# Value projections of two attention mixers in halves of 256 columns, two accumulator banks each, and earlier key fills

## The chip, the cores and the metric

The kernel runs as one program on one core of a Trainium2 chip. The metric is the device time of one execution in microseconds (us). The profile names the engines PE (TensorE: matrix products), PEld (its loads of the stationary operand), DVE (VectorE), ACT (ScalarE), POOL (GpSimd) and SP (SyncE, which issues most DMAs).

## The reference

A trunk of two layers works on x (512 positions, 1024 channels) with a memory of 256 positions, all in float32. Cut to what matters here:

```python
# layer 0, the first mixer
proj = rms_norm(x) @ attn_w_in            # 1024 -> 3080 columns
fq, fk, fv, ff, dq, dk, dv = split(proj)  # fv: 512 columns, 8 heads of 64
p = softmax(causal(fq @ fk.T / 8 + F[:, None] - F[None, :]))   # F = cumsum(log_sigmoid(ff))
fox_out = p @ fv
d_out = rms_norm((softmax(mask(dq1 @ dk1.T)) - lam * softmax(mask(dq2 @ dk2.T))) @ dv)
x = x + concat(fox_out, d_out) @ attn_w_out
# layer 1, the second mixer
qk, v, ig, fg, og = split(rms_norm(x) @ mlstm_w_in)   # v: 1024 columns, 4 heads of 256
q, k = split(silu(causal_depthwise_conv(qk)))         # 4 heads of 128
num, den = gated_causal_sums(q, k, v, ig, fg)         # chunkwise in the reference
h = rms_norm(num / max(abs(den), exp(-m)))            # by heads
x = x + (h * sigmoid(og)) @ mlstm_w_out
# both layers, behind the mixer
x = x + memory_cross_attention(rms_norm(x), rms_norm(mem))
x = x + conv_ffn(rms_norm(x))                         # 1024 -> 2 x 2816 -> 1024
```

A last rms_norm follows. The output is 512 x 1024.

## The kernel before

**Precision.** Each operand of a matrix product is split into a high and a low part (`hi = cast(v)`, `lo = v - hi`), and a product is three matmuls: high by high, high by low, low by high. In projections with channels in the partitions these are lines 388, 389 and 390 (`mm3`), in the value projections (tokens in the partitions, `p_proj_tok`) lines 450, 451 and 452. Each weight tile is 128 x 1024 (512 KB). SP loads it into `raw` (three buffers), ACT casts it to `wh`, DVE subtracts to `wl`. Nearly every operation of ACT and DVE is recorded at line 310, the wrapper that keeps an engine's operations in order, so the names of its tiles tell them apart.

**Order.** The two mixers are written as items for a planner (class `Plan`, line 86). An item has a priority (lower goes first), items that it depends on, and resources that it takes and frees: two banks for scores ("s"), two for weighted sums and transposes ("w"), four accumulator banks ("acc"), three weight slots ("wt"), and buffers such as "v" and "qk". The plan keeps a clock of ACT and DVE and lists the items one by one; in that order the instructions go out on each engine, and each engine keeps to it.

**First mixer** (`mix0`, line 876). The differential attention's four heads and the forgetting attention's eight heads, the latter in four pairs `p_` with priorities 50, 60, 70, 80. A pair's q and k projections (`p_qk`) give `qa` and `ka`; scores (lines 798 and 799; `kb` carries a bias part) go to an "s" bank; the softmax is POOL's bias, DVE's sums (`sm`) and ACT's exponentials, DVE scales `x` by 1/sum; PE transposes x into `w` (line 831) and a copy makes `pt`; line 1068 multiplies pt by the values v. The values of all eight heads are one projection 512 wide, `p_values` (line 847) with priority 49: eight steps over the channels of 12 matmuls 128 x 512, in four accumulator banks, one for each 128 tokens. A pair's weighted sum waits for all four.

Then come the output projection (`wo0`, eight blocks of 24 matmuls of 512 columns, which read `mh`/`ml`, `ka`, `qa`, the parts of the mixer's output) with priority 100, and the key fills (`p_fill`, line 1140): two blocks of the memory's keys, for the cross-attention that follows, four weights with 24 matmuls of 256 columns each, with priority 99 and not before 210 us on the planner's clock.

**Second mixer** (from line 2100). Gates, four heads with priorities 10, 20, 30, 40. A head's q and k blocks (24 matmuls of 512 each) go through a convolution on DVE and ACT (`hs`, `cv`, `th`) to `q`, `ql`, `k`, `kl`; scores `s<-q,k`, masked to `at`; denominators by `w<-hsq,ones` (line 2254); numerators `w<-at,v` (line 2275) go to `num`; their squares `hsq` are summed on PE (line 547), and the root comes back through a DMA as `hrb`, by which DVE scales num. The gates' columns are transposed at line 2132 (`s<-ident,cv`). The values are two projections of 512 columns (two heads each) in four banks: the first with priority 2, ahead of all heads, the second with 31, and a head's numerators wait for its projection, `ves[h // 2]`.

The rest of each layer (cross-attention, ConvFFN) is ordered by another class and isn't touched.

## Time and profile before

| | |
|---|---|
| median of 3 runs | 1406.63 us (1406.47 to 1407.09) |
| profiled execution, its own time | 1407.05 us |
| its span | 1404.9 us |
| granted TensorE clock | 1.00 |
| busy: PE, PEld | 1390.2 us (99%), 1265.2 us (90%) |
| busy: DVE, ACT, POOL | 1186.4 us (84%), 874.4 us (62%), 146.8 us (10%) |
| DMA | 211.06 MB, mean 150 GB/s |

The profile is of one execution, and its own time is 0.42 us above the median; the span is the part from the first to the last recorded instruction. [...] In square brackets behind a row stands how long the engine idled before it and what released it. "out<-in" gives the tiles by their names in the program, "128*128 128x512" the shape of the stationary operand and of the result.

### The profile page before, as it was taken

How to read it: one execution, taken by the hardware profiler on the slowest of the kernel's cores; microseconds unless marked ns; L12 is line 12 of the kernel's file. 1: busy time of each engine (PE TensorE's matmuls, PEld its weight loads, DVE VectorE, ACT ScalarE, POOL GpSimd, SP SyncE). 2: the span in 40 equal slices, each digit the busy share in tenths (PEclk: the TensorE clock that was granted, in tenths of full speed). 3: DMA queues.
4: the chain of work that ended last, by engine and by line, in shares of the span. 5: the costliest groups of instructions: out<-in, count | busy, mean ns of one | idle time of the engine just before them, and what ended most of it. 6: DMA issues, size and time to landing. Idle time of an engine off the chain costs nothing.

```text
span 1404.9 us, 23512 instructions
## 1 busy us (share of the span) xinstructions
PE 1390.2 (99%) x8876; PEld 1265.2 (90%) x8876; DVE 1186.4 (84%) x2042; ACT 874.4 (62%) x1486; POOL 146.8 (10%) x213
## 2 busy tenths in 40 slices
PE   9999999999999999999999999999999999999998
PEld 8888878899899999999888888989989999999997
DVE  7787786888799999999768876678878999999984
ACT  6797565666576665666456664456656866565555
POOL 0002230010011111011001120001000111110000
PEclk9999999999999999999999999999999999999999
DMA  6225324765567787674333332367464878776522
GB/s 207 91 53 154 117 68 151 246 188 158 158 145 191 211 199 187 151 200 106 86 108 105 129 98 83 120 188 240 136 185 114 196 201 204 182 185 168 154 66 81
DMA packets 80544, 211.06 MB, mean 150 GB/s; under 512 B 8640, under 2 KB 8640, under 8 KB 80432
## 3 DMA queue, kind: packets, MB, share of 16 engines
q1 hardware_dynamic: 63520, 165.02, 36.3%
q0 software_dynamic: 15904, 43.44, 17.7%
q8 instruction: 69, 1.13, 0.3%
q10 hardware_dynamic: 1008, 1.12, 0.2%
q14 instruction: 43, 0.35, 0.1%
HBM read 203.20 MB, written 6.34 MB: 149 GB/s over the span
## 4 chain that ended last, share of the span: by engine, by line
PE 85%; DVE 8%; ACT 3%; issue 2%; DMA 1%; POOL 1%; SPq 0%; POOLq 0%; DVEq 0%; ACTq 0%
PE acc L388 16%; PE acc L390 16%; PE acc L389 16%; PE w L388 4%; PE w L389 4%; PE w L390 4%; PE s L388 3%; PE s L390 3%; PE s L389 3%; PE acc L451 2%; PE acc L452 2%; PE acc L450 2%; DVE wl L310 1%; DVE qc L310 1%; PE w L2275 1%
## 5 line engine op out<-in xcount | busy, mean ns | idle before, releaser
L310 ACT CAST wh<-raw 128x1024 fp32r<-128x1024 f32 (+2 forms) x217 | 222.0, 1026 | 160.9 <-PE acc L389 76.4
L310 DVE TENSOR_TENSOR wl<-raw,wh 128x1024 fp32r<-128x1024 f32 (+2 forms) x217 | 259.6, 1198 | 39.2 <-ACT wh L310 37.9
L388 PE MATMUL acc<-xh,wh 128*128 128x256 f32 (+1 forms) x704 | 228.7, 325 | 0.0
L390 PE MATMUL acc<-xh,wl 128*128 128x256 f32 (+1 forms) x704 | 227.4, 323 | 0.5 <-DVE wl L310 0.5
L389 PE MATMUL acc<-xl,wh 128*128 128x256 f32 (+1 forms) x704 | 227.1, 323 | 0.0
L390 PEld LDWEIGHTS acc<-xh,wl 128*128 128x128 f32 x704 | 134.4, 191 | 9.3 <-DVE wl L310 0.9
L388 PEld LDWEIGHTS acc<-xh,wh 128*128 128x128 f32 x704 | 134.5, 191 | 7.6
L389 PEld LDWEIGHTS acc<-xl,wh 128*128 128x128 f32 x704 | 134.5, 191 | 7.5
L310 DVE SCALAR_TENSOR_TENSOR qc<-va,vec,qc 128x512 f32<-128x512 f32 x176 | 131.8, 749 | 6.9 <-ACT qc L310 4.0
L389 PE MATMUL acc<-f,k 128*128 128x256 f32 x336 | 92.5, 275 | 0.0
L390 PE MATMUL acc<-f,k 128*128 128x256 f32 x336 | 92.5, 275 | 0.0
L388 PE MATMUL acc<-f,k 128*128 128x256 f32 x336 | 92.5, 275 | 0.0
L310 ACT ACTIVATE qc<-va,vec 128x512 f32<-128x512 f32 x88 | 71.1, 812 | 19.2 <-DVE q L310 9.5
L388 PE MATMUL w<-q,wh 128*128 128x512 f32 x208 | 79.1, 380 | 0.6 <-ACT qc L310 0.6
L390 PE MATMUL w<-q,wl 128*128 128x512 f32 x208 | 78.9, 379 | 0.0
L389 PE MATMUL w<-q,wh 128*128 128x512 f32 x208 | 78.9, 379 | 0.0
L310 ACT ACTIVATE u<-acc 128x256 f32<-128x256 f32 x96 | 36.4, 379 | 68.1 <-PE acc L390 66.4
L390 PE MATMUL acc<-mem,wl 128*128 128x256 f32 (+1 forms) x236 | 73.8, 313 | 1.1 <-DVE wl L310 1.1
L388 PE MATMUL acc<-mem,wh 128*128 128x256 f32 (+1 forms) x236 | 73.9, 313 | 0.1
L389 PE MATMUL acc<-mem,wh 128*128 128x256 f32 (+1 forms) x236 | 73.7, 312 | 0.0
L310 DVE TENSOR_TENSOR x<-acc,x 128x512 f32<-128x512 f32 (+1 forms) x43 | 28.0, 653 | 47.2 <-PE acc L390 47.2
L310 ACT CAST k<-xe 128x512 fp32r<-128x512 f32 x84 | 51.0, 614 | 25.4 <-DVE xe L310 10.7
(414 smaller groups left out, 4207.0 us busy)
## 6 DMA issues: line engine op xcount, KB each, us to landing
raw<-in_up_dram SPq DMA_DIRECT2D x46, 512.0 KB, 4.3
raw<-in_down_dram SPq DMA_DIRECT2D x32, 512.0 KB, 4.6
sa<-in_up_dram SPq DMA_DIRECT2D x28, 512.0 KB, 5.1
sa<-in_up_dram POOLq DMA_DIRECT2D x28, 512.0 KB, 6.5
vb<-in_up_dram SPq DMA_DIRECT2D x42, 256.0 KB, 4.0
xe<-in_up_dram POOLq DMA_DIRECT2D x42, 256.0 KB, 4.8
raw<-in_wo_dram SPq DMA_DIRECT2D x16, 512.0 KB, 3.6
raw<-in_xk_dram SPq DMA_DIRECT2D x16, 512.0 KB, 3.9
```

The costliest lines, as they stand in the source:

```text
L310: i = issue(*a, **k)
L388: mm(out, wh, xh, start=first, stop=False, skip_group_check=parts)
L389: mm(out, wh, xl, start=False, stop=False, skip_group_check=parts)
L390: mm(out, wl, xh, start=False, stop=last, skip_group_check=parts)
L450: mm(ps, xh[k][:, ts], wh, start=(k == 0), stop=False)
L451: mm(ps, xh[k][:, ts], wl, start=False, stop=False)
L452: mm(ps, xl[k][:, ts], wh, start=False, stop=(k == 7))
L2275: nc.tensor.matmul(ps[:, lo:], vv[s][:, c], a[:], start=(s == 0), stop=(s == 3))
```

## The change

The forgetting attention's values and the second mixer's values go through a new function, `p_half`, in place of `p_values` and `p_proj_tok`. A half is 256 columns of values. Two blocks of 128 tokens share one bank, so a half takes two accumulator banks instead of four, a step over 128 channels is 12 matmuls of 256 columns, and one weight tile holds four steps instead of two. ACT empties each block by itself, 128 x 256.

The first mixer has two halves, with priorities 57 and 77: the first behind the first pair's softmaxes (55), the second behind the third pair's (75), where banks and weights allow it. Pairs 0 and 1 wait for the first half, pairs 2 and 3 for the second. (The differential attention's values stay 512 wide.) The second mixer has four halves, one for each head, with priorities 2, 15, 31 and 41, and a head waits for its own alone. The host lays the weights out to suit. The time before which the first mixer's fills may not begin falls from 210 to 185 us on the planner's clock.

```diff
--- before.py
+++ after.py
@@ -30,9 +30,10 @@
 WARM = 12
 ROW_DMA, SPREAD_DMA, LATE = 2.7, 6.0, 12.0
 DECAY_AT = 90.0
+FOX_V_PRIO, HEAD_V_PRIO = (7, 27), (2, 15, 31, 41)
 MEM_AT, MEM_STEP = (140.0, 100), (24.0, 16.0)
-FILLS, FILL_AT, FILL_PRIO = 2, (210.0, 140.0), 99
-SOFT_PRIO, OGATE_PRIO, V1_PRIO = 5, 18, 31
+FILLS, FILL_AT, FILL_PRIO = 2, (185.0, 140.0), 99
+SOFT_PRIO, OGATE_PRIO = 5, 18
 BIG = 1e30
 BANKS = {"s": ("s", 2), "b": ("s", 2), "w": ("w", 2), "t": ("w", 2)}
 
@@ -844,6 +845,47 @@
             self.nc.tensor.matmul(ps[:, j * P : 512], v[j][:, cols], pt[:, at : at + 512 - j * P], start=(j == 0), stop=(j == 3))
         return ps
 
+    def p_half(self, pl, src, out, half, edeps, prio, kdeps=None, tag="v"):
+
+        st = {}
+        last = None
+        take = (tag,) if tag and half == 0 else ()
+        cs = slice(256 * half, 256 * half + 256)
+        for k in range(KB8):
+
+            def fn(k=k):
+                c, k2 = divmod(k, 4)
+                if k2 == 0:
+                    st["w"] = self.weight(src[c])
+                if k == 0:
+                    st["ps"] = [self.acc_bank(b) for b in st["banks"]]
+                (wh, wl), (xh, xl) = st["w"], self.xs()
+                mm = self.nc.tensor.matmul
+                ws = slice(256 * k2, 256 * k2 + 256)
+                wh, wl = alternate(wh[:, ws]), alternate(wl[:, ws])
+                for t in range(4):
+                    ps = banked(st["ps"][t // 2][:, 256 * (t % 2) : 256 * (t % 2) + 256])
+                    ts = slice(t * P, (t + 1) * P)
+                    mm(ps, xh[k][:, ts], wh, start=(k == 0 and t % 2 == 0), stop=False, skip_group_check=True)
+                    mm(ps, xh[k][:, ts], wl, start=False, stop=False, skip_group_check=True)
+                    mm(ps, xl[k][:, ts], wh, start=False, stop=(k == 7), skip_group_check=True)
+
+            first = k % 4 == 0
+            last = pl.add(
+                fn, 12 * 0.111, [last, *(kdeps or {}).get(k, [])], prio,
+                take=(("acc", "acc") if k == 0 else ()) + (("wt",) if first else ()),
+                free=("wt",) if k % 4 == 3 else (), pre=(("A", 0.95), ("D", 1.14)) if first else (), st=st,
+            )
+
+        def evac(b):
+            for t in (2 * b, 2 * b + 1):
+                if out[t] is None:
+                    out[t] = self.til(self.mp, "v", bufs=8)
+                ps = st["ps"][b][:, 256 * (t % 2) : 256 * (t % 2) + 256]
+                self.nc.scalar.activation(out[t][:, cs], ps, AF.Identity, scale=self.r[:, t : t + 1])
+
+        return [pl.add(lambda b=b: evac(b), 0, [last, *edeps], prio, take=take if b == 0 else (), free=("acc",), chain=(("A", 0.82),), st=st) for b in range(2)]
+
     def p_values(self, pl, src, edeps, prio, kdeps=None, ready=None):
 
         out = [None] * 4
@@ -1019,8 +1061,9 @@
             for p_ in range(4):
                 p = 50 + 10 * p_
                 if p_ == 0:
-                    v, ve = self.p_values(pl, t["fv"], [norm], p - 1, xk)
-                    used = []
+                    v, used = [None] * 4, []
+                    ves = [self.p_half(pl, t["fv"][i], v, i, [norm], p + FOX_V_PRIO[i], xk) for i in range(2)]
+                ve = ves[p_ // 2]
                 st, qk = self.p_qk(pl, t["fq"][p_], t["fk"][p_], p_ % 2, xk, [norm], p)
                 ss = []
                 kd[p_] = []
@@ -2139,14 +2182,7 @@
             uc = pl.add(ucols, 0.4, [pl.add(lambda: None, 0, [g], 2, chain=(("-", 3.0),))], 2, take=("s",), free=("s",), chain=(("D", 0.1),))
 
             v = [[None] * 4, [None] * 4]
-            ves = []
-            for nh in range(2):
-
-                def values(tk, ps, nh=nh):
-                    v[nh][tk] = self.til(mp, "v", bufs=8)
-                    nc.scalar.activation(v[nh][tk][:], ps, AF.Identity, scale=self.r[:, tk : tk + 1])
-
-                ves.append(self.p_proj_tok(pl, t["mv"][nh], self.xs, 4, values, edeps=[norm], prio=2 if nh == 0 else V1_PRIO))
+            ves = [self.p_half(pl, t["mv"][h], v[h // 2], h % 2, [norm], HEAD_V_PRIO[h], tag=None) for h in range(4)]
 
             def conv(ps, blk, scale, tag):
                 hs = self.til(mp, "hs", (P, 576), bufs=1)
@@ -2282,7 +2318,7 @@
                             nc.scalar.activation(th[:], nm[:], AF.Square)
                         nc.vector.tensor_tensor(out=st["sq"][:], in0=st["sq"][:], in1=th[:], op=ALU.add)
 
-                    a = pl.add(nums, 2.14, xs_ + ves[h // 2] + [de], p + 1, take=("w",), free=("w",) + (("at",) if d else ()), chain=(("A", 0.5),))
+                    a = pl.add(nums, 2.14, xs_ + ves[h] + [de], p + 1, take=("w",), free=("w",) + (("at",) if d else ()), chain=(("A", 0.5),))
                     ns.append(pl.add(lambda: None, 0, [a], p + 1, chain=(("A", 0.52), ("D", 0.6))))
 
                 def scaled(rb, h=h, st=st):
@@ -2438,14 +2474,14 @@
     a["mem"] = row_chunks(i["mem"][0].T)
     w = i["attn_w_in"][0]
     a["fq"], a["fk"] = col_blocks(w[:, FOX_Q:FOX_K]), col_blocks(w[:, FOX_K:FOX_V])
-    a["fv"] = row_chunks(dealt(w[:, FOX_V:FOX_F]))
+    a["fv"] = np.stack([row_chunks(dealt(w[:, FOX_V + n : FOX_V + n + 256])) for n in (0, 256)])
     a["gate0"] = w[:, FOX_F:DIF_Q].reshape(KB8, P, 8).transpose(1, 0, 2)
     a["dq"], a["dk"] = col_blocks(w[:, DIF_Q:DIF_K]), col_blocks(w[:, DIF_K:DIF_V])
     a["dv"] = row_chunks(dealt(w[:, DIF_V:]))
     a["wo0"] = col_blocks(i["attn_w_out"][0])
     w = i["mlstm_w_in"][0]
     a["mqk"] = col_blocks(w[:, :1024])
-    a["mv"] = np.stack([row_chunks(dealt(w[:, 1024:1536])), row_chunks(dealt(w[:, 1536:2048]))])
+    a["mv"] = np.stack([row_chunks(dealt(w[:, 1024 + n : 1280 + n])) for n in range(0, 1024, 256)])
     a["gate1"] = w[:, 2048:2056].reshape(KB8, P, 8).transpose(1, 0, 2)
     a["mog"] = col_blocks(w[:, 2056:])
     a["wo1"] = col_blocks(i["mlstm_w_out"][0])
```

PE has 8851 rows of instructions in place of 8562; DVE, POOL and SP have as many as before, ACT 1399 in place of 1382. Lines move by one behind the new constants (389, 390 and 391 are the three matmuls of `mm3`) and by 43 behind `p_half` (1111 for 1068).

PE at the end of the first mixer, before: the last pair's weighted sum is followed by its share of three blocks of the output projection (`acc_380`, `acc_391`, `acc_437`), and then by the fills (`acc_512`, from `mem`).

```order
L389 MATMUL acc_380_1851<-qa_508_2409,wh_1846 128x512
L390 MATMUL acc_380_1851<-qa_507_2408,wl_1847 128x512
L389 MATMUL acc_391_1892<-qa_508_2409,wh_1887 128x512
L390 MATMUL acc_391_1892<-qa_507_2408,wl_1888 128x512
L389 MATMUL acc_437_2070<-qa_508_2409,wh_2065 128x512
L390 MATMUL acc_437_2070<-qa_507_2408,wl_2066 128x512
L388 MATMUL acc_512_2421<-mem_1593,wh_2416 128x256
L389 MATMUL acc_512_2421<-mem_1593,wh_2416 128x256
L390 MATMUL acc_512_2421<-mem_1593,wl_2417 128x256
L388 MATMUL acc_512_2421<-mem_1598,wh_2416 128x256
L389 MATMUL acc_512_2421<-mem_1598,wh_2416 128x256
L390 MATMUL acc_512_2421<-mem_1598,wl_2417 128x256
```

The fills stand behind all steps of the attention; the output projection's other five blocks come behind them.

PE in the last pair's part after: the first of the fills' blocks (`acc_444`, from `mem`) begins among scores (`s`), transposes (`w<-ident,x`) and steps of two blocks of the output projection (`acc_383`, `acc_396`).

```order
L799 MATMUL s_2329<-ka_325_1700,qa_322_1691 128x512
L800 MATMUL s_2329<-kb_116,qa_322_1691 128x512
L389 MATMUL acc_396_2018<-mh_129,wh_2013 128x512
L390 MATMUL acc_396_2018<-ml_135,wh_2013 128x512
L391 MATMUL acc_396_2018<-mh_129,wl_2014 128x512
L799 MATMUL s_2338<-ka_431_2134,qa_428_2126 128x256
L800 MATMUL s_2338<-kb_115,qa_428_2126 128x256
L832 MATMUL w_2218<-ident,x_144 128x128 x4
L389 MATMUL acc_444_2183<-mem_1781,wh_2229 128x256
L390 MATMUL acc_444_2183<-mem_1781,wh_2229 128x256
L1111 MATMUL w_2246<-pt_1872,v_1246 64x512
L1111 MATMUL w_2246<-pt_2025,v_1246 64x512
```

The fills have moved in front of the last pairs' weighted sums, and the transposes of x_144 follow a pair of scores directly.

PE at the end of the first mixer after, behind the last weighted sum (`w_2593`):

```order
L1111 MATMUL w_2593<-pt_2503,v_1252 64x128
L389 MATMUL acc_383_1969<-qa_517_2602,wh_1964 128x512
L389 MATMUL acc_396_2018<-qa_517_2602,wh_2013 128x512
L390 MATMUL acc_383_1969<-qa_518_2603,wh_1964 128x512
L391 MATMUL acc_383_1969<-qa_517_2602,wl_1965 128x512
L390 MATMUL acc_396_2018<-qa_518_2603,wh_2013 128x512
L391 MATMUL acc_396_2018<-qa_517_2602,wl_2014 128x512
L389 MATMUL acc_525_2628<-mh_127,wh_2623 128x512
L390 MATMUL acc_525_2628<-ml_133,wh_2623 128x512
L391 MATMUL acc_525_2628<-mh_127,wl_2624 128x512
```

Two blocks of the output projection instead of three were begun beforehand, and a third (`acc_525`) stands where the fills stood.

PE in the second mixer before, where head 1's k block (`acc_1489`) ends and head 0's first scores (`s_8555`) begin:

```order
L389 MATMUL acc_1489_8525<-xl_1398_8106,wh_8520 128x512
L390 MATMUL acc_1489_8525<-xh_1397_8105,wl_8521 128x512
L388 MATMUL acc_1489_8525<-xh_1400_8122,wh_8520 128x512
L389 MATMUL acc_1489_8525<-xl_1401_8123,wh_8520 128x512
L390 MATMUL acc_1489_8525<-xh_1400_8122,wl_8521 128x512
L388 MATMUL s_8555<-q_8411,k_8457 128x512
L389 MATMUL s_8555<-ql_8412,k_8457 128x512
L390 MATMUL s_8555<-q_8411,kl_8458 128x512
L388 MATMUL s_8566<-q_8411,k_8457 128x384
L389 MATMUL s_8566<-ql_8412,k_8457 128x384
```

And after, where the scores of head 0 (`s_8737`) stand in the k block of head 1:

```order
L389 MATMUL acc_1489_8725<-xh_1363_8023,wh_8720 128x512
L390 MATMUL acc_1489_8725<-xl_1364_8024,wh_8720 128x512
L391 MATMUL acc_1489_8725<-xh_1363_8023,wl_8721 128x512
L389 MATMUL acc_1489_8725<-xh_1370_8055,wh_8720 128x512
L390 MATMUL acc_1489_8725<-xl_1371_8056,wh_8720 128x512
L391 MATMUL acc_1489_8725<-xh_1370_8055,wl_8721 128x512
L389 MATMUL s_8737<-q_8490,k_8536 128x512
L390 MATMUL s_8737<-ql_8491,k_8536 128x512
L391 MATMUL s_8737<-q_8490,kl_8537 128x512
L389 MATMUL s_8748<-q_8490,k_8536 128x384
```

Head 0's scores now come two steps into head 1's k block instead of behind it; the second half of the values (`acc_1464` and `acc_1465`) stands in between, ahead of head 1's q block.

DVE in the second mixer before, at the adds to head 1's squares (`hsq`) and the scaling of head 0's num by hrb:

```order
L310 COPY mk_9050<-at_1576_8937 128x128
L310 TENSOR_TENSOR hsq_8958<-hsq_8958,th_8995 128x512
L310 TENSOR_TENSOR at_1603_9039<-s_9035,mk_9030 128x128
L310 TENSOR_TENSOR mk_9050<-mk_9050,at_1603_9039 128x128
L310 TENSOR_TENSOR hsq_8958<-hsq_8958,th_9014 128x512
L310 TENSOR_TENSOR hs_9073<-acc_1587_8975,rb_8235 128x512
L310 TENSOR_TENSOR hsq_9056<-mk_9050,cv_9055 128x512
L310 TENSOR_SCALAR z_9069<-s_9064 128x4
L310 SCALAR_TENSOR_TENSOR num_8872<-num_8872,vec,hrb_9062 128x512
L310 SCALAR_TENSOR_TENSOR cv_9076<-hs_9073,vec,cv_9076 128x512
```

And after:

```order
L311 TENSOR_TENSOR wl_9329<-raw_9327,wh_9328 128x1024
L311 SCALAR_TENSOR_TENSOR num_9007<-num_9007,vec,hrb_9218 128x512
L311 SCALAR_TENSOR_TENSOR num_9017<-num_9017,vec,hrb_9218 128x512
L311 TENSOR_TENSOR num_9007<-num_9007,sg_8844 128x512
L311 TENSOR_TENSOR num_9017<-num_9017,sg_8910 128x512
L311 TENSOR_TENSOR mixed_9368<-num_9007,mixed_9367 128x512
L311 TENSOR_TENSOR mixed_9373<-num_9017,mixed_9372 128x512
L311 TENSOR_TENSOR hsq_9091<-hsq_9091,th_9189 128x512
L311 TENSOR_TENSOR hsq_9091<-hsq_9091,th_9201 128x512
L311 TENSOR_TENSOR wl_9419<-raw_9417,wh_9418 128x1024
L311 TENSOR_SCALAR z_9252<-s_9247 128x4
```

Six operations of the scaled num, which begin with the wait for hrb, have moved ahead of the last two adds to hsq.

## The prediction

> **What bounds the kernel now.** I read the page first, its busy times and its chain:
>
> ```profile
> span 1404.9 us, 23512 instructions
> PE 1390.2 (99%) x8876; PEld 1265.2 (90%) x8876; DVE 1186.4 (84%) x2042; ACT 874.4 (62%) x1486; POOL 146.8 (10%) x213
> PE 85%; DVE 8%; ACT 3%; issue 2%; DMA 1%; POOL 1%; SPq 0%; POOLq 0%; DVEq 0%; ACTq 0%
> ```
>
> TensorE (PE) is busy 99% of the span, and 85% of the chain that ended last is its work. So only two things can move the time: PE work that is added, and the few moments in which PE stands. DVE is the next engine. The span is one profiled execution whose own time is 1407.05 us; the median of the runs is 1406.63, 0.42 below it. I make the sum against 1407.05 and take 0.42 off at the end. A measurement of this kernel can tell about 0.2%, 2.8 us, from no change.
>
> Next the busy times by stretch (columns: stretch, its length and then PE, PEld, DVE, ACT, POOL busy, clock, DMA share, GB/s), for the stretches that the change touches:
>
> ```profile
> 90.00:120.00 30.00, 29.60 (x143) 23.79 (x142) 26.94 (x83) 25.43 (x60) 2.03 (x4) 1.00 0.31 92
> 120.00:170.00 50.00, 49.95 (x263) 43.80 (x262) 38.25 (x90) 35.48 (x68) 15.18 (x25) 1.00 0.49 138
> 170.00:217.00 47.00, 43.88 (x247) 31.38 (x246) 37.67 (x125) 27.83 (x71) 12.27 (x24) 1.00 0.24 74
> 740.00:820.00 80.00, 78.44 (x373) 65.91 (x372) 67.63 (x109) 54.27 (x84) 14.96 (x32) 1.00 0.37 116
> 820.00:900.00 80.00, 80.00 (x420) 69.09 (x419) 52.82 (x80) 37.61 (x53) 6.78 (x10) 1.00 0.32 99
> ```
>
> PE idles 0.40 + 0.05 + 3.12 us in the first mixer and 1.56 in the second: 5.1 us in all, and that is nearly all that a better order can win. The granted clock is 1.00 everywhere, so it plays no part. DMA is busy half of the time or less, and the change loads the same bytes in as many tiles, so I cost the loads at nothing.
>
> **Part 1: twice as many matmuls, half as wide.** Each value product of 512 columns becomes two of 256: 96 of them in the first mixer (the forgetting attention's), 192 in the second. What a pair costs beyond the one it replaces is in the PE timeline (start, duration, engine, line): the key fills are 256 wide, the output projection behind them is 512 wide, and both run without a wait.
>
> ```profile
> 216.77 0.28 PE L388 MATMUL acc<-mem,wh 128*128 128x256 f32 x1
> 227.05 0.28 PE L390 MATMUL acc<-mem,wl 128*128 128x256 f32 x1
> 227.16 0.38 PE L388 MATMUL acc<-mh,wh 128*128 128x512 f32 x1
> 252.85 0.38 PE L390 MATMUL acc<-qa,wl 128*128 128x512 f32 x1
> ```
>
> 216.77 is the fourth of the 96 fill matmuls and 227.05 the last: 92 steps in 10.28 us, 0.1117 each. From 227.16 to 252.85 are five blocks of 24, 119 steps in 25.69 us, 0.2159 each. (The durations overlap; start to start is the cost.) 2 x 0.1117 - 0.2159 = 0.0075 us a pair; 288 pairs are **+2.2 us**, 0.7 in the first mixer and 1.5 in the second. PE is the bound, so this lies on the path whole.
>
> [...]
>
> The evacuations: ACT empties 24 tiles of 256 columns where it emptied 12 of 512. By the rows below that is 24 x 0.379 - 12 x 0.694 = +0.8 us on ACT, which is busy 62%: PE's work hides it, and uncovered it would cost 0.8.
>
> ```profile
> L310 ACT ACTIVATE v<-acc,y 128x512 f32<-128x512 f32 x8 | 5.0, 694 | 2.2 <-PE acc L452 2.2
> L310 ACT ACTIVATE u<-acc 128x256 f32<-128x256 f32 x96 | 36.4, 379 | 68.1 <-PE acc L390 66.4
> ```
>
> **Part 2: the key fills go into the first mixer's tail.** Before, they follow the chain's last step, the last pair's contribution to the output projection:
>
> ```profile
> 209.09 2.85 PE L1068 MATMUL w<-pt,v 128*64 128x512 f32 x16
> 212.62 0.92 PE L388 MATMUL acc<-qa,wh 128*128 128x512 f32 x3 [0.68 <-ACT qa L310]
> 214.53 0.38 PE L390 MATMUL acc<-qa,wl 128*128 128x512 f32 x1
> 214.98 0.38 PE L388 MATMUL acc<-mem,wh 128*128 128x256 f32 x1
> 215.19 0.28 PE L389 MATMUL acc<-mem,wh 128*128 128x256 f32 x1
> 216.56 0.38 PE L390 MATMUL acc<-mem,wl 128*128 128x256 f32 x1 [1.09 <-DVE wl L310]
> ```
>
> From 214.53 to 216.77 lie one step of 512 and three of 256, 0.55 us of work, in 2.24 us: 1.7 us are lost because DVE splits the fill's weights too late. After, what follows the last qa is a block of the output projection whose split stands far ahead in DVE's order, so this goes: I take **-1.6**, between -1.7 and 0 (the split late again). The 0.68 wait for qa stays, since the last weighted sum is again followed at once by steps that read qa.
>
> The price is on DVE. Four fill weights are split among the last heads' softmaxes:
>
> ```profile
> L310 DVE TENSOR_TENSOR wl<-raw,wh 128x1024 fp32r<-128x1024 f32 x37 | 45.1, 1224 | 10.8 <-ACT wh L310 10.6
> 180.10 0.38 PE L798 MATMUL s<-ka,qa 128*128 128x256 f32 x1 [0.38 <-DVE sm L310]
> 185.10 0.63 PE L831 MATMUL w<-ident,x 128*128 128x128 f32 x4 [0.18 <-DVE x L310]
> 186.06 0.43 PE L798 MATMUL s<-ka,qa 128*128 128x384 f32 x1 [0.33 <-DVE sm L310]
> ```
>
> Four splits are 4 x 1.224 = 4.9 us in a stretch where DVE has 47.00 - 37.67 = 9.3 free and PE already waits for it at scores and transposes. Against that stand 10.7 us of fill matmuls (96 x 0.1117) that PE can do while DVE works. Queued behind a split on DVE are the softmax sums, the scaling of x and the copies to pt, and for those the transposes and the next scores wait. After, the transposes of x_144 come right behind the scores, with no fill matmul ahead of them. I take **0**: what the fills cover, the splits delay. The ends are -1.3 (idle of the stretch without the 0.68 and the 1.09, all gone) and +4.9 (every split delays PE by its length).
>
> **Part 3: the forgetting attention's values spread out.** Before, first scores are wedged between the 512 wide value matmuls:
>
> ```profile
> 90.41 0.38 PE L451 MATMUL acc<-wl,xh 128*128 128x512 f32 x1
> 91.18 0.43 PE L798 MATMUL s<-ka,qa 128*128 128x384 f32 x1 [0.40 <-DVE sm L310]
> 91.98 0.38 PE L799 MATMUL s<-kb,qa 128*128 128x512 f32 x1
> ```
>
> 90.41 to 91.98 hold steps of 512, 384, 384 and 512 columns, 2 x 0.216 + 2 x 0.165 = 0.76 us of work in 1.57: 0.8 lost to the softmax sums. After, two pairs of scores at most are followed by 12 half-wide matmuls, 1.3 us, before the next, and the second half lies among later scores, so they come less densely. I take **-0.8**, with 0 as the other end (the same wait elsewhere). What is late next is again a softmax sum, in the tail.
>
> **Part 4: the second mixer's values by heads.** Three waits stand here:
>
> ```profile
> 742.10 0.38 PE L390 MATMUL acc<-xh,wl 128*128 128x512 f32 x1
> 742.63 0.41 PE L2132 MATMUL s<-ident,cv 4*128 4x4 f32 x4
> 762.71 0.38 PE L390 MATMUL acc<-xh,wl 128*128 128x512 f32 x1
> 763.91 0.48 PE L388 MATMUL s<-q,k 128*128 128x512 f32 x1 [0.82 <-ACT k L310]
> 816.34 0.38 PE L390 MATMUL acc<-xh,wl 128*128 128x512 f32 x1
> 817.28 1.03 PE L547 MATMUL s<-ones,hsq 128*128 128x2 f32 x8 [0.56 <-DVE hsq L310]
> ```
>
> Less one step of 0.216 each, they lose 0.31, 0.98 and 0.72: 2.0 us.
>
> The first goes: the gate columns' transposes now stand some 4 us of PE work later behind their gates. So does the second: between the end of head 0's key projection and its scores stood head 1's q and k blocks and two more steps, 50 steps or 10.8 us. Now half 1 (10.7), the q block (5.2) and six steps of the k block (1.3) stand there, 17.2 us. The third also goes: 3.9 us of matmuls cover the squared norms, in place of 2.35. **-2.0** together.
>
> New waits can come. By the rows above the chain from the key projection to a ready kl took 10.8 + 0.98, about 12 us:
>
> ```profile
> 754.59 0.69 DVE L310 TENSOR_TENSOR hs<-acc,rb 128x512 f32<-128x512 f32 x1
> 763.89 0.69 DVE L310 SCALAR_TENSOR_TENSOR kl<-cv,k 128x512 fp32r<-128x512 f32 x1
> ```
>
> In DVE's order these are the ends of a conv that other work interleaves. After, head 1's scores have only 9.5 us of PE work behind their key projection. If the conv takes as long again, they wait 2.3 us; if DVE, relieved of the gates by then, runs it in 9.5, nothing. I take **+1.0**. At the mixer's end the cover of the last denominators' chain falls from 9.2 to 5.2 us of matmuls; the nearest price is the wait of 0.82 above, the lower end zero, and I take **+0.3**. One more risk is in DVE's order: a scaling of num by hrb, which waits for a DMA trip, now stands ahead of the last adds to hsq:
>
> ```profile
> 809.84 0.95 PE L547 MATMUL s<-ones,hsq 128*128 128x2 f32 x8
> 819.24 0.97 DVE L310 SCALAR_TENSOR_TENSOR num<-num,vec,hrb 128x512 f32<-128x512 f32 x1
> ```
>
> The trip took 9.4 us before. After, about 10.7 us of PE work lie between the two, so it should be there 1.3 us early: 0, and up to +0.8 if not.
>
> **The sum.** 1407.05 + 2.2 - 1.6 + 0 - 0.8 - 2.0 + 1.0 + 0.3 = 1406.15; less 0.42, **1405.7 us**. The uncertain terms taken together give this case 1403.4 to 1408.0 as its own range.
>
> **The rivals.**
>
> *All waits go.* The halves and fills may cover DVE everywhere. Then the 1.7, 0.8 and 2.0 go, and the tail's 1.3 of idle, which by starts is about twice that (as 0.8 against 0.40 at 91.18), 2.6: -7.1 + 2.2 from 1407.05, less 0.42: 1401.7. For it speaks that PE work is spread to where PE waits; against it, DVE's 80% in the tail and 85% in 740:820, which leave little room to run ahead.
>
> *Slower: the splits bind the tail.* DVE and PE go in step in the tail: a score, its softmax, a transpose, a copy, the weighted sum. If the splits stand between these on DVE, each delays the next transposes. It decides when three of the four splits delay PE whole, since 3 x 1.22 = 3.7 us above the forecast is 1409.4. All four give 1405.7 + 4.9 = 1410.6. Against it stands the 9.3 us that DVE has free there; for it, the transposes of x_144 behind DVE's queue.
>
> *The weight load binds at 256 columns.* Each half-wide matmul needs its own load. The page has
>
> ```profile
> L390 PEld LDWEIGHTS acc<-xh,wl 128*128 128x128 f32 x704 | 134.4, 191 | 9.3 <-DVE wl L310 0.9
> ```
>
> If 0.191 could not hide under the shorter matmul, a pair would cost 0.382 - 0.216 = 0.166 more, and 288 of them 48 us: 1454. The fills at 0.1117 with a load each speak against it. [...]
>
> *The fills do not come sooner.* They may only start when acc banks and a weight slot are free, so they may run where they did. Then 1.6 stays: 1407.3. The order of instructions speaks against it.
>
> **How the numbers follow.** The forecast 0.46, all waits go 0.28, the tail bound by splits 0.16, fills no sooner 0.08, the weight load 0.02. Faster by over 0.2% (under 1403.8) is the second case and 0.08 of the forecast's lower end: 0.36. Slower (over 1409.4) is 0.14 of the third case and the 0.02: 0.16. The rest is 0.48. The range goes from 1401.0 to 1410.6: it takes in the case where all waits go and that of all four splits, and leaves out some 0.06 below and 0.08 above.
>
> **What would show it.** Value halves that step at 0.112 in the changed profile; no wait for wl at the first matmuls behind the last qa; the idle PE time of the first mixer's tail, and whether w<-ident,x or s<-ka,qa there wait for DVE longer than 0.4; s<-q,k without a wait for head 0 and with about 1 us for head 1. The forecast is wrong if halves step at more than 0.12, if the tail's waits grow by more than 2 us, or if PE stands still for under 2 us over both mixers.

## The result and the profile after

The changed kernel takes **1417.13 us** (1416.66 to 1420.38) beside 1406.61 (1406.47 to 1407.09) for the kernel before: a ratio of 1.0079, 95% interval 1.0064 to 1.0094. It is 10.5 us slower, outside the range and on the side that had the smallest chance. The profiled execution took 1416.93 us. The page's rows of after:

```profile
span 1415.2 us, 24080 instructions
PE 1393.7 (98%) x9164; PEld 1277.9 (90%) x9164; DVE 1184.9 (84%) x2042; ACT 873.1 (62%) x1498; POOL 149.8 (11%) x213
PE 80%; DVE 10%; ACT 4%; issue 2%; DMA 1%; POOL 1%; POOLq 0%; SPq 0%; ACTq 0%; DVEq 0%
```

By these rows PE has 288 instructions more than before, one for each split product, and ACT 12, one for each added evacuation. The span grew by 10.3 us, but PE's busy time by only 3.5; in the chain PE fell from 85% to 80%, and DVE and ACT rose by 2 and 1. So most of the loss is waiting. The busy times by stretch of after (columns as before: length, PE, PEld, DVE, ACT, POOL, clock, DMA share, GB/s) say where:

```profile
90.00:120.00 30.00, 30.00 (x199) 28.00 (x198) 24.71 (x68) 25.12 (x55) 0.53 (x1) 1.00 0.23 75
120.00:140.00 20.00, 16.75 (x76) 12.99 (x76) 15.78 (x43) 16.15 (x34) 5.14 (x9) 0.91 0.51 152
140.00:170.00 30.00, 29.53 (x197) 26.95 (x196) 21.90 (x54) 17.67 (x37) 8.58 (x13) 1.00 0.46 135
740.00:800.00 60.00, 58.83 (x329) 51.65 (x328) 50.00 (x80) 39.81 (x64) 10.31 (x21) 1.00 0.38 119
800.00:815.00 15.00, 12.71 (x88) 11.81 (x88) 9.30 (x16) 6.88 (x11) 3.67 (x6) 0.89 0.48 130
```

Two short stretches carry it: 120 to 140 us in the first mixer, where PE idles 3.25 us (0.05 between 120 and 170 before), and 800 to 815 in the second, where it idles 2.29. In both, and apart from the last microsecond of the kernel only there, the granted clock is below 1.00. So each holds two losses, one behind the other. The first mixer on PE:

```profile
125.24 0.38 PE L391 MATMUL acc<-xh,wl 128*128 128x512 f32 x1
126.76 2.42 PE L845 MATMUL w<-pt,v 128*128 128x512 f32 x8 [1.15 <-ACT pt L311]
...
131.06 0.38 PE L391 MATMUL acc<-xh,wl 128*128 128x512 f32 x1
133.54 0.44 PE L832 MATMUL w<-ident,x 128*128 128x128 f32 x2 [2.11 <-DVE pt L311]
...
134.62 0.64 PE L389 MATMUL acc<-xh,wh 128*128 128x512 f32 x1
135.05 0.63 PE L390 MATMUL acc<-xl,wh 128*128 128x512 f32 x1
...
138.01 0.38 PE L391 MATMUL acc<-xh,wl 128*128 128x512 f32 x1
```

By starts, less a step of 0.216, the waits are 1.31 us (125.24 to 126.76) and 2.27 (131.06 to 133.54). Then, from 134.62 to 138.01, eight steps of 512 columns take 3.39 us where they take 1.73 at full clock: half speed, another 1.66. Who is late is in the timelines of ACT, SP and DVE:

```profile
117.42 1.05 ACT L311 CAST wh<-raw 128x1024 fp32r<-128x1024 f32 x1
122.47 1.04 ACT L311 CAST wh<-raw 128x1024 fp32r<-128x1024 f32 x1 [4.00 <-DMA raw<-in_fv_dram]
123.42 0.61 ACT L311 CAST ka<-tmp 64x512 fp32r<-64x512 f32 x1
...
126.24 0.47 ACT L311 COPY pt<-w 128x384 f32<-128x384 f32 x1
```

```profile
118.93 2.79 SPq L311 DMA_DIRECT2D raw<-in_fv_dram  x2
```

```profile
117.72 1.19 DVE L311 TENSOR_TENSOR wl<-raw,wh 128x1024 fp32r<-128x1024 f32 x1
...
122.63 0.54 DVE L311 CUSTOM_DVE_ANT_0 x<-s,dmask 128x384 f32<-128x384 f32 x1
```

ACT stands 4.00 us for the first weight of the values' second half. SP issues that load at 118.93, when DVE has split the third pair's q weights (117.72 to 118.91) and so freed their raw buffer. Behind ACT's cast are queued ka, qa, the softmaxes' x and the copies to pt; the wait of 1.15 ends with the copy at 126.24. But DVE is late too: from 114 to 124 it works without a listed wait, and the softmax sums that ACT's exponentials of x need are only begun at 122.63. How much of PE's loss is the load's is a question for the experiments. The second mixer, PE and then DVE of after:

```profile
801.48 0.28 PE L871 MATMUL acc<-wh,xl 128*128 128x256 f32 x1
801.59 0.95 PE L548 MATMUL s<-ones,hsq 128*128 128x2 f32 x8
...
803.38 0.28 PE L871 MATMUL acc<-wh,xl 128*128 128x256 f32 x1
805.94 0.48 PE L2290 MATMUL w<-hsq,ones 128*128 128x512 f32 x1 [2.29 <-DVE hsq L311]
...
807.31 0.42 PE L871 MATMUL acc<-wh,xl 128*128 128x256 f32 x1
807.52 0.42 PE L869 MATMUL acc<-wh,xh 128*128 128x256 f32 x1
```

```profile
800.62 0.69 DVE L311 TENSOR_TENSOR hsq<-hsq,th 128x512 f32<-128x512 f32 x1 [0.54 <-ACT th L311]
802.02 0.68 DVE L311 TENSOR_TENSOR hs<-acc,rb 128x512 f32<-128x512 f32 x1
802.62 1.21 DVE L311 TENSOR_TENSOR wl<-raw,wh 128x1024 fp32r<-128x1024 f32 x1
803.75 1.53 DVE L311 SCALAR_TENSOR_TENSOR cv<-hs,vec,cv 128x512 f32<-128x512 f32 x2
805.20 0.69 DVE L311 TENSOR_TENSOR hsq<-mk,cv 128x512 fp32r<-128x512 f32 x1
...
814.95 1.41 DVE L311 SCALAR_TENSOR_TENSOR num<-num,vec,hrb 128x512 f32<-128x512 f32 x2 [3.26 <-DMA hrb<-roots]
...
819.89 0.69 DVE L311 TENSOR_TENSOR hsq<-hsq,th 128x512 f32<-128x512 f32 x1 [0.94 <-ACT th L311]
```

There is one hsq buffer. Head 0's squares fill it until PE reads them at 801.59; only then can the low part of head 1's sums go into it, and by then DVE has 3.4 us of other work (hs, wl, cv) in front of that step. PE waits 2.46 by starts, and steps of 256 columns then take 0.21 us in place of 0.11. In the kernel before the same buffer held up the same step, but there DVE stood ready for it (PE reads the squares at 809.84), and PE used the result at 811.58 without a wait:

```profile
810.83 0.69 DVE L310 TENSOR_TENSOR hsq<-mk,cv 128x512 fp32r<-128x512 f32 x1 [0.76 <-PE s L547]
```

What PE loses can be summed over the span: the distance from start to start, less the full-clock step of that kind of matmul. After it loses 8.0 us more than before. The first mixer has 3.9 of these (2.0 less than before up to 120 us, 5.6 more at 120 to 140, 0.3 more behind it) and the second 4.1. The other 2.3 us of the span are the width.

### The profile page after: what moved, and what is told of

Read it like the earlier page. It is cut to its first block, busy times and chain, and to the rows that moved or that the text cites. A ratio compares the mean times of both kernels' runs of the same rounds, so it can differ in the third digit from the quotient of the medians.

```text
span 1415.2 us, 24080 instructions
## 1 busy us (share of the span) xinstructions
PE 1393.7 (98%) x9164; PEld 1277.9 (90%) x9164; DVE 1184.9 (84%) x2042; ACT 873.1 (62%) x1498; POOL 149.8 (11%) x213
## 3 DMA queue, kind: packets, MB, share of 16 engines
q8 instruction: 72, 1.18, 0.3%
## 4 chain that ended last, share of the span: by engine, by line
PE 80%; DVE 10%; ACT 4%; issue 2%; DMA 1%; POOL 1%; POOLq 0%; SPq 0%; ACTq 0%; DVEq 0%
PE acc L389 16%; PE acc L391 16%; PE acc L390 16%; PE w L389 4%; PE w L390 4%; PE w L391 4%; PE s L389 3%; PE s L391 3%; PE s L390 3%; DVE wl L311 2%; DVE qc L311 1%; PE acc L1429 1%; PE acc L1430 1%; PE acc L1431 1%; DVE cv L311 1%
## 5 line engine op out<-in xcount | busy, mean ns | idle before, releaser
L389 PEld LDWEIGHTS acc<-f,k 128*128 128x128 f32 x336 | 64.4, 192 | 0.8
L390 PEld LDWEIGHTS acc<-f,k 128*128 128x128 f32 x336 | 64.4, 192 | 0.8
```

The source lines that it names most:

```text
L389: mm(out, wh, xh, start=first, stop=False, skip_group_check=parts)
L390: mm(out, wh, xl, start=False, stop=False, skip_group_check=parts)
```

## Experiments

Two theories stood first. **Order**: the values moved between waits that no longer have cover, and in-order engines stand for something late. **Width**: 256 columns cost more than their steps show.

**Width alone**: the kernel before, each value matmul as two of 256, in place.

```diff
-                    mm(ps, xh[k][:, ts], wh, start=(k == 0), stop=False)
...
+                    for h in range(2 if narrow else 1):
+                        z = slice(128 * h, 128 * h + 128) if narrow else slice(0, n // 2)
+                        po, ph, pl_ = ps[:, z], wh[:, z], wl[:, z]
...
```

> The kernel before, with each value matmul of 512 columns of the forgetting attention and of the second mixer done as two of 256 in the same place and the same bank; nothing else moves. Theory A (two blocked queues: the halves themselves cost only their cadence, and the rest of the 10.5 us comes from where they stand): 288 pairs x 0.0075 = +2.2 us, 1408.8 us, granted clock 1.00 in every stretch. Theory B (the width itself: 256-column streams cost more than the fills showed, or lower the clock): most of the 10.5 us is here already, 1414 us or more, with stretches of lower clock in the value projections.

1411.69 us, 1.0037 (1.0023 to 1.0050): between the two. Its PE timeline shows why:

```profile
766.76 0.48 PE L388 MATMUL s<-q,k 128*128 128x512 f32 x1 [1.98 <-ACT k L310]
...
769.30 0.63 PE L389 MATMUL acc<-xl,wh 128*128 128x512 f32 x1
769.73 0.63 PE L390 MATMUL acc<-xh,wl 128*128 128x512 f32 x1
```

The wait for k, 0.82 before, became 1.98, because the scheduler orders ACT and DVE anew around the doubled instructions, and half clock follows it (0.43 a step, some 1.7 us in all). Take these 2.9 off, and 2.2 for the steps is what is left of the span's +5.4 but for 0.3. Width is what was forecast; a reordering costs more than it.

**Each mixer alone, and the fills alone**: the change with the second mixer as before (first), with the first mixer as before (second), and the kernel before with only the fills' new time (third).

```diff
-    a["mv"] = np.stack([row_chunks(dealt(w[:, 1024 + n : 1280 + n])) for n in range(0, 1024, 256)])
+    a["mv"] = np.stack([row_chunks(dealt(w[:, 1024:1536])), row_chunks(dealt(w[:, 1536:2048]))])
...
-    a["fv"] = np.stack([row_chunks(dealt(w[:, FOX_V + n : FOX_V + n + 256])) for n in (0, 256)])
+    a["fv"] = row_chunks(dealt(w[:, FOX_V:FOX_F]))
...
-FILLS, FILL_AT, FILL_PRIO = 2, (210.0, 140.0), 99
+FILLS, FILL_AT, FILL_PRIO = 2, (185.0, 140.0), 99
```

> The changed kernel with the second mixer as before (two projections of 512 columns); the first mixer's halves and earlier fills stay. Theory A: 0.7 for the width and 4.4 net for the waits that stand between 120 and 230 us in the changed kernel's trace, +5.1, 1411.7 us; one dip of the clock, at about 134 to 138 us, behind a wait of 2.3 us. Theory B (width): a third of the matmuls, +3.5, 1410.1 us, with no dip that follows a wait.

1411.06, 1.0034 (1.0021 to 1.0047), near theory A's time, but without its dip: the two waits stand at 125 and 131 (0.97 and 2.28 by starts), and no half clock follows. PE then waits 1.78 at 151 instead, where after has 0.63.

> The changed kernel with the first mixer as before (one projection of 512 columns, fills not before 210); the second mixer's four halves stay. Theory A: 1.5 for the width and 4.0 net for the waits from 740 to 900 us, +5.5, 1412.1 us, with one dip of the clock behind a wait of about 2.5 us for hsq. Theory B: two thirds of the matmuls, +7.0, 1413.6 us.

1414.34, 1.0055 (1.0038 to 1.0071), above both forecasts. Both mixers lose by themselves, and their losses (4.7 and 8.0) do not simply add up to the 10.5 of the whole change. On PE:

```profile
775.93 0.48 PE L389 MATMUL s<-q,k 128*128 128x512 f32 x1 [1.02 <-ACT k L311]
777.80 0.80 PE L391 MATMUL s<-q,kl 128*128 128x512 f32 x1 [1.18 <-DVE kl L311]
...
803.03 0.48 PE L2289 MATMUL w<-hsq,ones 128*128 128x512 f32 x1 [0.89 <-DVE hsq L311]
819.96 1.05 PE L548 MATMUL s<-ones,hsq 128*128 128x2 f32 x8 [2.51 <-DVE hsq L311]
```

Here the low part's wait is short and that for the squares long: the same two waits for hsq that the next group takes apart, differently shared.

> The kernel before with the first mixer's fills allowed from 185 us on the planner's clock, nothing else. Theory C (what counts is where in-order engines stand): the 1.7 us at the fills' hand-over go and the splits inside the tail give some of it back, -1.5 to 0, 1404.7 to 1406.2 us. Rival (the fills in the tail make DVE the bound): +1 to +4, 1407 to 1410 us.

1407.38, 1.0007 (0.9997 to 1.0016): nothing that can be told from zero. The hand-over's wait is gone, but the last heads wait for pt instead:

```profile
185.72 0.30 PE L831 MATMUL w<-ident,x 128*128 128x128 f32 x1 [0.61 <-DVE x L310]
208.13 2.37 PE L1068 MATMUL w<-pt,v 128*64 128x512 f32 x16 [1.10 <-DVE pt L310]
```

The prediction's -1.6 came, and its 0 for the tail was +1.6 or a little more.

**The second mixer**: first the sums' low part gets a tile of its own kind; then, besides, the scaling of num is put behind the next head's adds on DVE (in front of which it stood for hrb).

```diff
-                    st["d"] = [self.til(mp, "cv", dtype=F32R)[:], self.til(mp, "hsq", dtype=F32R, bufs=1)[:]]
+                    st["d"] = [self.til(mp, "cv", dtype=F32R)[:], self.til(mp, "th", dtype=F32R)[:]]
...
+                        if h and d:
+                            far[1]["behind"] = nc.vector.last
...
+                    if h and d:
+                        far[0].order = [a]
```

> The changed kernel with one tile renamed in the second mixer: the low part of a head's sums goes to a buffer of th instead of the only buffer of hsq, which the previous head's squares hold until PE has summed them. In DVE's order the subtraction then stands ahead of the next key's convolution instead of between its taps. Theory A (the 2.46 us wait of w<-hsq,ones and the 1.7 us of half clock behind it come from that place in DVE's queue): the wait falls under 0.5, the dip goes, -4.2, 1413.0 us. Rival (DVE is behind here in any order, since it has too much work): the wait stays above 1.5 here or at the next instruction, 1416 to 1417 us.

1421.70, 1.0108 (1.0093 to 1.0124): slower still, which both theories had wrong. The wait for the low part is gone; behind it (DVE, then PE)

```profile
818.71 1.42 DVE L311 SCALAR_TENSOR_TENSOR num<-num,vec,hrb 128x512 f32<-128x512 f32 x2 [3.33 <-DMA hrb<-roots]
...
825.14 0.69 DVE L311 TENSOR_TENSOR hsq<-hsq,th 128x512 f32<-128x512 f32 x1 [0.84 <-ACT th L311]
```

```profile
825.88 1.87 PE L548 MATMUL s<-ones,hsq 128*128 128x2 f32 x8 [3.20 <-DVE hsq L311]
```

DVE stands 3.33 us for hrb's DMA with the adds to hsq behind it, and PE waits for those adds. In after, the wait at 805.94 had hidden this one. That is not the whole of it: against after, the second mixer loses 2.2 us more and the first 3.7, though the edit leaves the first mixer's order as it was. There the profile shows no half clock at 134, but a wait of 2.59 at 152 (0.63 in after), half clock behind it (0.21 us a step of 256 columns), and again at 197 (over 180 to 260 us the granted clock was 0.98).

> The kernel with the renamed tile, and DVE's scaling of a head's num by hrb put behind the next head's two adds to hsq instead of ahead of them. Theory C: the 3.4 us wait at s<-ones,hsq, in which DVE stood 3.3 us for hrb, and the 1.7 us of half clock behind it go: -4 to -5 against the renamed tile alone (1421.7), 1417 us, and 1413 us where the first mixer's POOL stand is short as in the changed kernel's profile. Rival (DVE has too much work in this stretch in any order): the wait moves to the next score or sum, and no more than 1 us is won, 1420 to 1422 us.

1416.80, 1.0073 (1.0058 to 1.0088): 4.9 us under the run before it, as expected. The wait at s<-ones,hsq and its half clock are gone (from 800 to 830 us PE loses 0.2 in place of 5.5), so the stand for hrb is shown as their cause. But beside the changed kernel's 1417.13 the two edits together win only 0.3 here: in this profile PE also waits 1.2 for head 1's k, half clock follows at 783 (the granted clock of the whole execution was 0.997), and the first mixer, which they leave alone, loses 1.0 more than in after.

> The second mixer's halves alone (the first mixer as before), with the renamed tile and the adds ahead of the scaling. Theory C for the second mixer (its loss is the two queue places on DVE): 1414.3 of the halves alone less 4 to 6, 1408.5 to 1410.5 us: the 1.5 us of the width and 1 to 2 for the keys of the first two heads. Rival: 1412 us or more.

1410.07 (1407.97 to 1411.87), 1.0024 (1.0015 to 1.0034), as expected: both edits take 4.3 us off the second mixer's change by itself, so its loss is shown to be these two places in DVE's queue. PE's long waits for hsq are gone, and that for head 1's kl, 1.18, is the longest left in that mixer.

> The kernel before with the renamed tile and the adds ahead of the scaling. Here no convolution stands in front of hsq and no scaling in front of the adds, so there is little to win: theory C 1405.5 to 1407 us. Rival (the two edits help by themselves, whatever the halves do): 1404 us or less.

1407.00, 1.0002 (0.9992 to 1.0012): in the kernel before the two edits are worth nothing. They mend what the change made, and are no gain of their own.

> The changed kernel with the priority of the third head's half at 25 instead of 31, so that it stands ahead of the third head's q and k blocks and the convolutions come behind the sums of the second head. Theory C: no tap of a convolution stands ahead of hsq on DVE, so the 2.5 us wait and its half clock go, -4, 1413 us, if no other stand takes their place. Rival (the halves cost what they cost wherever they stand): 1416 to 1418 us.

1423.81, 1.0123 (1.0105 to 1.0141) with `HEAD_V_PRIO` at (2, 15, 25, 41): 11 us above theory C and 6 above the rival. PE waits 1.66 for k at 783 and 2.54 for hsq at 902.6 in place of the two waits meant to go.

**The first mixer**: is it the load, ACT that stands for it, or DVE's work? The memory's step begins at 125 in place of 140 (first); DVE casts the late weight, not ACT (second); the half moves up right behind the first (third) or behind the second pair (fourth).

```diff
-MEM_AT, MEM_STEP = (140.0, 100), (24.0, 16.0)
+MEM_AT, MEM_STEP = (125.0, 100), (24.0, 16.0)
...
+        self.nc.vector.tensor_copy(hi[:], raw[:])
...
-FOX_V_PRIO, HEAD_V_PRIO = (7, 27), (2, 15, 31, 41)
+FOX_V_PRIO, HEAD_V_PRIO = (7, 8), (2, 15, 31, 41)
```

> The changed kernel with the first layer's memory taken in at 125 instead of 140 on the planner's clock, which puts its load one place earlier in SP's order and lets the second value half reuse the memory's buffer instead of that of the third pair's q weights. Theory C (in-order queues that stand for a late arrival): ACT's 4.0 us stand at about 118 us for the second half's first weight goes down to 1 us or less, the waits of 1.3 and 2.3 us behind it and the half clock go, -4 to -5, 1412 to 1413 us. Rival (the load is late because the DMA engines are full, 0.9 to 0.99 busy at 120 to 128 us): ACT still stands 2 us or more, 1416 to 1417 us. Either way the POOL queue's stand at 148 us may add up to 3.5 us, as in the run with the renamed tile.

1429.03, 1.0158 (1.0142 to 1.0174), 16 us above theory C. The weight's load was issued at 120.62, no sooner than in after, so this is no test of an early load. ACT stands 3.93 us for it and 1.95 more for the memory's second load, and PE waits 3.20 at 131, with half clock behind it: up to 139.53 a step of 512 columns takes 0.43 us.

> The changed kernel with one cast moved: the high part of the second value half's first weight is written by DVE instead of ACT. ACT then has nothing to wait for at 118 to 122 us, whatever the load does. Theory C: the 4.0 us stand of ACT is what delays the copies to pt and the exponentials, so the waits of 1.3 and 2.3 us and the half clock of the first mixer go, -3 to -5, 1412 to 1414 us. Rival (the late load delays PE through the weight itself or through DVE): the wait stays, 1416 to 1418 us.

1419.93, 1.0095 (1.0079 to 1.0110): the rival. ACT no longer stands for the load, and DVE only 0.44 us; yet ACT stands 3.09 at 124 for DVE's softmax sums, and PE waits 1.58 and 1.34 for DVE's pt. ACT's stand for the load is not the cause.

> The changed kernel with the first mixer's second half right behind the first (priority 58 instead of 77); fills and second mixer as changed. Theory D (the values were PE work that asks nothing of DVE and ACT; with half of them moved away, the second pair's q and k, whose outputs DVE and ACT must scale, cast and copy, come 10 us sooner among the differential heads' softmaxes, and both engines fall behind): the waits and the half clock at 120 to 140 us, 5.4 us in the changed kernel, fall under 1, and what comes later in the mixer decides the rest: 1411 to 1414 us. Rival (the late load of the half's weight makes them): the load is as late as before in SP's order or goes with it; no more than 2 us of them go, or they move with the half.

1422.73, 1.0111 (1.0096 to 1.0126), 9 us above theory D; PE has lost 6.9 us by 140, where after had lost 5.6. The fv load is early now, and others are late in its place. ACT's timeline, and the busy times at 120 to 140:

```profile
122.62 1.05 ACT L311 CAST wh<-raw 128x1024 fp32r<-128x1024 f32 x1 [1.94 <-DMA raw<-in_fq_dram]
131.10 0.42 ACT L311 ACTIVATE sqt<-raw 128x256 f32<-128x256 f32 x1 [3.54 <-DMA raw<-in_mem_dram]
```

```profile
120.00:140.00 20.00, 17.20 (x75) 13.58 (x74) 10.56 (x32) 12.50 (x28) 7.11 (x11) 0.83 0.51 158
```

DVE is busy 10.56 us of 20 and ACT 12.50: here they are not overloaded, they stand.

> The changed kernel with the first mixer's second half at priority 67, behind the second pair's q and k and ahead of the third pair's. Theory D: the second pair's q and k come as soon as in the changed kernel, so the waits at 120 to 140 us stay at 2 us or more, though the half is there to fill some of them and the third pair's q and k come later: 1413 to 1418 us. Rival (the late load): the half's weight is asked for sooner, and the waits go, 1411 us or less.

1423.35, 1.0115 (1.0100 to 1.0130): the waits of 1.25 and 2.3 stay, as theory D has them, and more come behind (2.73 at 194, and 2.33 and 2.68 in the second mixer), which put the time above both forecasts. Yet the half's two weights were loaded early here, at 92.34 and 111.00. ACT stands as long as in after, now for the third pair's q weights, whose load is issued at 119.19:

```profile
122.72 1.05 ACT L311 CAST wh<-raw 128x1024 fp32r<-128x1024 f32 x1 [4.00 <-PE w L832]
```

The profile names PE as what ended this stand. But the cast begins 3.53 us after the load's issue, and in after 3.54, so I put it down to the load. So what is late at this place is the next load in SP's order, whichever weight that is.

A last one takes the load out of the queue for the three raw buffers: it goes to two tiles that hold the memory's parts only later, at the program's start, by POOL.

```diff
+            self.nc.gpsimd.dma_start(raw[:], src[:, s].bitcast(F32R))
+            self.split(hi[:, s], lo[:, s], v)
...
+                    ves = [self.p_half(pl, t["fv"][i], v, i, [norm], p + FOX_V_PRIO[i], xk, home=(mh[1], ml[1]) if i else None) for i in range(2)]
```

> The changed kernel, with the first weight of the first mixer's second half loaded at the program's start into two 128x512 tiles that hold the memory's high and low parts only later, so that this load needs none of the three raw buffers, and the loads behind it move up by one. If the first mixer's waits at 120 to 140 us come from late weight loads, the two waits there (1.15 and 2.1 us in the changed kernel) and the half clock behind them (about 1.7 us) shrink to under 1 us together, and the time falls from 1417 to 1411.5 to 1413. If they come from the order of DVE's and ACT's work, over 2 us of waits stay in that stretch, and the time is 1415 to 1420.

1417.70, 1.0089 (1.0072 to 1.0106): the time is the rival's, the stage half of each. Busy times, PE, POOL and ACT:

```profile
120.00:140.00 20.00, 17.93 (x89) 14.19 (x88) 17.60 (x46) 16.23 (x35) 4.97 (x9) 1.00 0.42 133
```

```profile
127.03 2.42 PE L845 MATMUL w<-pt,v 128*128 128x512 f32 x8 [0.43 <-ACT pt L311]
...
133.11 0.44 PE L832 MATMUL w<-ident,x 128*128 128x128 f32 x2 [1.41 <-DVE pt L311]
...
151.43 0.48 PE L799 MATMUL s<-ka,qa 128*128 128x512 f32 x1 [1.96 <-DVE sm L311]
```

```profile
149.71 0.54 POOL L311 DMA_DIRECT2D hrb<-roots  x1 [2.78 <-DMA roots<-y]
```

```profile
124.20 0.62 ACT L311 ACTIVATE x<-x,sm 128x384 f32<-128x384 f32 x1 [2.50 <-DVE sm L311]
```

The two waits shrink from 3.26 to 1.84 us, and the half clock goes: 2.8 us are lost at 120 to 140 in place of 5.5. So the early load takes 1.4 us off the waits at this place. That the half clock went with them proves little, as it stayed out of the first mixer alone too, at longer waits. What stays is not a load's: ACT has none to wait for and stands 2.50 us for DVE's softmax sums instead, and DVE and ACT are then busy 17.60 and 16.23 of 20 us.

In the time nothing is won: POOL stands 2.78 us for the DMA of the roots, DVE's next sums and PE's scores wait behind it, and PE's wait at 151 grows from 0.47 to 1.96. The first 80 us, where POOL now issues the load, lose 1.0 more. Up to 152 us PE has lost 6.1 us here, 6.3 in after, and 5.7 in the first mixer alone, at full clock; in the kernel before it was 2.3. So neither the late load nor the half clock decides when PE is past that point. What does is work that DVE, ACT and POOL hand on to one another, with the roots' DMA in it.

**All together**: the change with the early memory step and both second-mixer edits, with DVE's cast and both, with the load at the start and both; and the halves at the old places of the values, the fills at the old time.

> The changed kernel with the memory earlier, the renamed tile and the adds first. Theory C: both mixers' stands go, 1417.1 - 4.5 - 4.2 = 1408.4 us, that is the kernel before plus the 2.2 us of the width; up to 3.5 more if the POOL queue stands long at 148 us. Rival (too much work, order does not matter): above 1413 us.

1425.70, 1.0136 (1.0119 to 1.0153): the rival's time, 3.3 under the same without the two edits.

> The changed kernel with the cast by DVE, the renamed tile and the adds ahead of the scaling. Theory C: the three edits add up, 1416.8 of the run with the adds first less 3 to 5, 1412 to 1414 us; with the POOL stand short, 1409 us. Rival: no better than the run with the adds first, 1416 us or more.

1416.57, 1.0068 (1.0052 to 1.0085): the rival's time too, 3.4 under the run with DVE's cast alone.

> The same early load with the two edits to the second mixer (the sums' low part in a tile of its own, the scaling behind the next head's adds). If late loads make the first mixer's waits, both costs go together, and 1407.5 to 1411.5 are left; the rest above the time before is the width's 2.2 us and what stands in the first mixer's tail. If the order makes them, it stays at 1413 to 1418.

1414.65, 1.0065 (1.0050 to 1.0080), as was expected if the order makes the first mixer's waits, and 3.1 under the run with the early load alone. It is the best of the whole change, 8.6 us over the kernel before measured beside it (1406.03).

> The changed kernel with all halves put back where the whole projections stood (priorities 49 and 49; 2, 2, 31 and 31) and the fills not before 210 us: halves in two banks, but not spread among the heads. Theory C: the 2.2 us of the width and what the new order of the queues adds, as in the run of the width alone, 1408.5 to 1411.5 us. Rival (two banks and 256 columns cost by themselves): 1414 us or more.

```diff
-FOX_V_PRIO, HEAD_V_PRIO = (7, 27), (2, 15, 31, 41)
+FOX_V_PRIO, HEAD_V_PRIO = (-1, -1), (2, 2, 31, 31)
```

1426.87, 1.0146 (1.0131 to 1.0161), 15 us above theory C. The waits at 120 to 140 are gone (PE has lost 1.2 us by 140, in after 5.6), which fits the moved half as their origin, but 146 to 200 has several of 1 to 1.8 us, and at the second mixer's end PE waits 3.38 for v:

```profile
915.71 0.70 PE L389 MATMUL acc<-v,wh 128*128 128x512 f32 x2 [3.38 <-ACT v L311]
```

Halves take other banks and evacuations than whole values even in the same place, and the scheduler deals out everything behind them anew. Why it is as slow as this stays open. No version beat the kernel before.

## Why the prediction was wrong

Without the width, the sum gave the first mixer -2.4 and the second -0.7. By starts they lost 3.9 and 4.1.

- **Width, +2.2**: right. Halves step at 0.112 (800.25 to 801.48, eleven steps in 1.23 us; the row at 801.48 is shown above), and the span has 2.3 us that no wait explains. The weight load did not bind.
- **The fills' hand-over, -1.6**: right at its place, since no wait for wl follows the last qa. **The tail, 0**: mis-sized. With the fills alone the two together gave nothing, so the tail took 1.6 or a little more back, the most of it by a wait for pt at 208. The copy to pt stands behind a split of the fills' weights there (DVE's wl at 206.65, for which DVE itself stood 1.00 us). It is the mechanism of the slower rival, but at a third of its price; that rival is not what made the kernel slower.
- **Part 3, -0.8, "with 0 as the other end (the same wait elsewhere)"**: this step failed. What it looked at came out better than forecast: the wait at 91 went, and up to 120 us PE loses 2.0 us less than before. But the other end was no bound, as PE then loses 5.6 more at 120 to 140. The step looked at the waits between which the values had stood, and not at what their place had done for the other engines: it was PE work during which DVE and ACT could get ahead. With the second half moved behind the third pair, DVE's softmax sums come at 122.63, and PE runs into waits for pt. With the halves at the old places it did not. A load was late as well, which "The change loads the same bytes in as many tiles, so I cost the loads at nothing" had ruled out: the bytes are the same, the time at which a buffer is free is not. But that is 1.4 us of the waits, and an early load moved nothing in the time.
- **Part 4, -2.0 and +1.0**: the first two waits went, the third (head 1's hsq) fell from 0.72 to 0.37, and head 1's kl came at 1.34 by starts, forecast 1.0. What failed is that the list of new waits was short. The low part of head 1's sums, which needs the only hsq buffer, was not on it: with hs, wl and cv in front of it on DVE it cost 2.46, and half clock 1.57 behind it. **The hrb risk, 0 to +0.8**: the point was right and the bound was not. The trip took 13.4 us (801.59 to 814.95), not 9.4, mostly because DVE came to its step z only 4.9 us after PE's sums began (806.47), before after 1.6 (811.44). With the low part out of the way, PE waited 3.36 us for the adds behind it.
- **"The granted clock is 1.00 everywhere, so it plays no part"**: failed. It held in the kernel before, where no wait of PE was over 1.3 us by starts. After, half clock took 1.66 us from PE in the first mixer and 1.57 in the second. The first hardly reached the end, as the first mixer alone, at full clock there, had lost only 0.6 us less by 152.

The second mixer's cause is thus shown, the first mixer's in part argued. What stays open there: which step of DVE's, ACT's or POOL's order holds PE back up to 152 (the second half right behind the first, which should have cured it, lost 6.9 us by 140); and the size of POOL's stand for the roots, which differed from 1.75 us in after to 2.78 with the load at the start, though the order there is the same.

## What to carry to other kernels

When PE is busy 99%, a reordering has little to win and each in-order queue to lose. For every step that moves, write down what the other engines did under its cover, which buffer it needs and who holds that, and what stands in front of it in each queue. Undo a new wait only with the next one in view, because removing the first (the hsq buffer) brought out a longer one (hrb) in front of the same matmuls, and removing the late load brought out the one at 151. And behind a new PE wait, read the granted clock as well: the two stretches of half clock in after took 1.66 and 1.57 us from PE, behind waits of 2.27 and 2.46.

## What the runs showed of the hardware

The granted clock fell to half behind some PE waits of 2.14 to 3.20 us (by starts), and behind two of 1.18 and 1.34 close together. In after it was at half from 134.56 to 137.97, behind a wait of 2.27, and from 806.98 to 810.40, behind one of 2.46. Width alone had it behind 2.14, and the second mixer alone behind the two of 1.18 and 1.34 (the matmul of 512 columns behind the first took 0.48 us, that behind the second 0.80; the granted clock was 0.83 over 774 to 784). The first mixer alone had a wait of 2.28 at the same place as after and kept its clock (steps of 0.216 behind it), and so did the kernel before, with no wait over 1.3 (the ends of the kernels are left out here: the granted clock is 0.50 from 1404.20 us in before and from 1414.56 in after). Each of the two stretches in after lasts 3.41 us. There are longer ones: some 6.9 us with the load at the start (a granted clock of 0.77 over 800 to 815), and over 8 with the memory earlier (rows at half speed from 130.73 to 139.53).

What decides whether half clock follows a wait was not shown. The length of the wait alone does not: 2.27 us had it in after, 2.28 in the first mixer alone had not, nor had 2.70 at 902.59 with the third half sooner (steps of 0.216 behind it). And executions of the same kernel differ: with the load at the start and both edits, they took 1416.98 us at a granted clock of 0.997 and 1413.84 at 1.000.
